# Grouping matrix products by width in the out-projection and the FFN of a Hymba-style decoder layer

## The chip, the core and the metric

The kernel runs on one core of one Trainium2 chip. The core has a matrix engine (TensorE, called PE in the profile; its loads of the stationary operand are a lane of their own, PEld), a vector engine (VectorE, DVE), an engine for activation functions (ScalarE, ACT), a general-purpose engine (GpSimd, POOL) and SyncE (SP), which issues most of the transfers. Each engine works through its own queue in program order and waits on semaphores for the others. The metric is the device time of one execution in microseconds (us); of several runs the median is taken.

## The reference

One decoder layer, float32, 256 tokens, model width 1024:

```python
h = rms_norm(x, norm1_g[l])
proj = h @ w_in[l]
...
x = x + jnp.concatenate([attn, conv], axis=-1) @ w_out[l]
h = rms_norm(x, norm2_g[l])
x = x + (jax.nn.silu(h @ w_gate[l]) * (h @ w_up[l])) @ w_down[l]
```

`attn` is softmax attention of 8 heads of width 64 with RMS-normed, rotated queries and keys (one block of 256 keys, so plain causal attention); `conv` is a gated causal convolution over 31 taps with layer norm and swish. `w_out` is 1024x1024, `w_gate` and `w_up` are 1024x2816, `w_down` is 2816x1024.

## The kernel before, in words

Activations are kept transposed, channels on the 128 partitions and the 256 tokens along the free axis. TensorE reads float32 operands in a rounded form (type fp32r), so each float32 operand is split into a rounded high part and a remainder, the low part. A product is then high times high, plus low weight times high activation, plus high weight times low activation.

**Weights.** They come in blocks of 2048 columns by DMA into `raw` (4 buffers) and are split in pieces of 1024 columns: ACT writes the high part `wh` (line 195), DVE the low part `wl` (line 199), 7 buffers of each. `feed` issues these some 4 pieces ahead of the products that use them.

**Three ways of multiplying.** In the input projection (line 609) all products have 512 moving columns. In the out-projection `mm3s` (line 223 on) takes the four channel tiles of one half and issues twelve 256-column products into a 256-column bank `po`: `wh` and `wl` against the high activations `mixh` in turn, then four `wh` against the low part `mixl`. In the FFN `mm2` (line 207) takes, per weight tile, one product of 512 columns, `wh` against high and low activations side by side (line 210), and one of 256 columns, `wl` against the high activations (line 211). The bank's two halves are added later by `halves` (ACT copies one half, DVE adds).

**The stretch around the change.** The out-projection runs in two halves (attention channels, then convolution channels), each with 8 output tiles d. After each d, DVE adds the bank to the residual `x2T` (line 671). In the second half `x2_task` follows: ACT writes the high part of the FFN's input `g` (line 645) and squares for the norm (647), POOL sums the squares (649), DVE writes the low part of `g` (line 652). The layer norm of the convolution (`bn_stats` to `nb`, lines 564 to 569), its transposes `cT` on TensorE and the split into `mixh` and `mixl` (lines 180, 181) lie inside the first half. Then the FFN: 22 column tiles f, each with 8 gate products into `fg` and 8 up products into `fu`; `norm2_task` puts two matrix steps among them, `pss` (sum of the squares over partitions, in f = 0) and `prb` (line 692, transposes of `wide`, the second norm's factor that DVE has just worked out, lines 685 to 688; between gate and up of f = 1). Last the down projection: 8 tiles d with 22 pairs of products each into `pd`; the last tile takes all its 512-column products in a row (line 764) and its 256-column ones after them into `pdl` (line 773).

**What sets the order.** Python generators (`spawn`, `step`) that are advanced at fixed places of the loops; `keep_order` then fixes the order on each engine as it was written. There are 4 banks of the kind `mm` in PSUM, taken in turn by `po`, `fg`, `fu` and `pd`.

Of the kernel before, what the change touches and what calls it, by code (L numbers as in the profile page):

```python
# [9 lines left out]
F32R = mybir.dt.float32r  # L10
# [3 lines left out]
ALU = mybir.AluOpType  # L14
AX = mybir.AxisListType

P = 128
D = 1024
T = 256
NT = T // P  # L20
KT = D // P
# [4 lines left out]
NF = FF // P  # L26
# [5 lines left out]
PIECE = 1024  # L32
# [4 lines left out]
LEAD = 4  # L37
# [87 lines left out]
def _build(nc, tc, t, ctx):  # L125
# [9 lines left out]
    def mm_bank(name, cols=512):  # L135
        return psum.tile([P, cols], F32, name=name, tag="mm", bufs=4)
# [16 lines left out]
    now = [0]  # L153

    def spawn(gen, wait=0):
        tasks.append([now[0] + wait, gen])

    def step():
        for task in list(tasks):
            while task in tasks and task[0] <= now[0]:  # L160
                try:
                    task[0] = now[0] + next(task[1])
                except StopIteration:
                    tasks.remove(task)
        now[0] += 1
# [37 lines left out]
    def wtile(col, width):  # L203
        j, c = divmod(col, PIECE)
        return [p[:, c:c + width] for p in pieces[j]]

    def mm2(out, w, both, start, stop):


        nc.tensor.matmul(out.rearrange("p (a q) -> p a q", a=2), w[0], both, start=start, stop=False)  # L210
        nc.tensor.matmul(out[:, 0:T], w[1], both[:, 0, :], start=False, stop=stop)  # L211

    def halves(out, bank, side):

# [8 lines left out]
    def mm3s(out, pairs):  # L223

        ops = [(l[a], r[0]) for l, r in pairs for a in range(2)] + [(l[0], r[1]) for l, r in pairs]
        for a, (l, r) in enumerate(ops):
            nc.tensor.matmul(out, l, r, start=a == 0, stop=a == len(ops) - 1)  # L227

    def seed(y, v):

# [41 lines left out]
        nc.tensor.matmul(warm[:, 0:T], zeros[:, 0:P], zeros, start=True, stop=True)  # L272


    xh = keep.tile([P, KT, T], F32R, name="xh", tag="big_h")
    xl = keep.tile([P, KT, T], F32R, name="xl", tag="big_l")
    def split_x(kt):
        nc.scalar.activation(xh[:, kt, :], xT[kt], AF.Copy, scale=g1[:, kt:kt + 1])
        yield
# [338 lines left out]
    mix = G["mix"] = [keep.tile([P, KT, T], F32R, name="mix" + s, tag="big_" + s) for s in "hl"]  # L618
    O = [None, None]
    for h in range(H):  # L620
        feed(unit // 2 + LEAD)
# [33 lines left out]
    for half in range(2):  # L655
        for d in range(KT):
            step()
            feed(off // PIECE + (LEAD if half == 0 or d < OUT_LATE else LEAD - 1))
            if half == 1 and d == 0:
                early_ctx.close()  # L660
                late = ffn["late"] = pool("late")
                xg = late.tile([P, 2, KT, T], F32R, name="g2")
                ffn["h"], ffn["l"] = xg[:, 0], xg[:, 1]
                ffn["acc"] = late.tile([P, T], F32, name="acc")
            b = mm_bank(f"po{half}{d}", T)
            pairs = []
            for a in range(4):
                pairs.append((wtile(off, P), [m[:, 4 * half + a, :] for m in mix]))
                off += P
            mm3s(b, pairs)  # L670
            nc.vector.tensor_tensor(x2T[:, d, :], b, x2T[:, d, :], op=ALU.add)
            if half:
                spawn(x2_task(d))

# [38 lines left out]
    for f in range(NF):  # L713
        pg = t_bank("fg2", "s") if f == 2 else mm_bank(f"fg{f}")
        pu = mm_bank(f"fu{f}")
        order = [(z, k) for z in range(2) for k in range(KT)]
        if f == 0:
            order = [(z, k) for z in range(2) for k in range(KT - 2)]
            order += [(z, k) for k in range(KT - 2, KT) for z in range(2)]
        for a, (z, k) in enumerate(order):  # L720
            if a % 4 == 0:
                if f == a == 0:
                    step()
                feed((off + a * P) // PIECE + LEAD)
                if f or a:
                    step()
            if f and a == 2 * KT // 2:
                spawn(glu_task(f, pg, pu))
                ffn["up"][f] = now[0] + 2
            w = wtile(off + (z * KT + k) * P, P)  # L730
            mm2((pg, pu)[z], w, xg[:, :, k, :], k == 0, k == KT - 1)
        if f == 0:
            spawn(glu_task(0, pg, pu), GLU0_WAIT)
            ffn["up"][0] = now[0] + GLU0_WAIT
        off += 2 * KT * P
# [15 lines left out]
    for d in range(KT):  # L751
        b = mm_bank(f"pd{d}")
        lows = []
        for f in range(NF):
            if f % 4 == 0:
                feed(off // PIECE + LEAD)
                step()
            w = wtile(off, P)
            off += P
            if d < KT - 1:  # L760
                mm2(b, w, acts[:, :, f, :], f == 0, f == NF - 1)
            else:
                both = b.rearrange("p (a q) -> p a q", a=2)
                nc.tensor.matmul(both, w[0], acts[:, :, f, :], start=f == 0, stop=f == NF - 1)  # L764
                lows.append(w[1])
        if d < KT - 1:
            for _ in out_task(d, b):
                pass
# [60 lines left out]
```

## Time and profile before

| | |
|---|---|
| median of 3 runs | 302.23 us (301.79 to 303.49) |
| profiled execution | 301.46 us, of which the span of the program's instructions is 299.3 us |
| PE busy | 292.5 us (98% of the span) |
| DVE busy | 222.6 us (74%) |
| ACT busy | 173.1 us (58%) |
| DMA | 56.6 MB, mean 189 GB/s |

Busy times are unions: matmuls overlap, so the busy time of a group is more than what it adds to the span. What a matmul adds is the distance from its start to the next one's. Rows of a timeline give the start in us from the span's start, the length, engine, line, operation, what is written from what, shapes, and in brackets the idle time before it with what ended it; consecutive equal rows are merged (x22), and then the length runs from the first start to the last end. In the chain of waits the length of a merged row is the time that it adds to the chain.

### The profile page before, as it was taken

To read this page: it belongs to the slowest core of one execution; us is meant where nothing else is said; L and a number is where in the kernel's file an instruction comes from. 1 tells how busy PE (TensorE), PEld (TensorE's weight loads), DVE (VectorE), ACT (ScalarE), POOL (GpSimd) and SP (SyncE) were. 2 spreads that over 40 slices of the span, in tenths; PEclk is the share of its full clock that TensorE was granted. 3 is DMA by queue.
4 is the path that set the end of the run, shared out by engine and by line. 5 is a ranking of instruction groups with operands and counts; after the bars stand their busy time and mean duration, and the time that the engine had idled before them with its cause. 6 is when DMAs were issued, how large, how long until landed. Compare 5 with 4: busy or idle time off the path is not lost.

```text
span 299.3 us, 4415 instructions
## 1 busy us (share of the span) xinstructions
PE 292.5 (98%) x1663; PEld 249.0 (83%) x1663; DVE 222.6 (74%) x414; ACT 173.1 (58%) x303; POOL 21.2 (7%) x41
## 2 busy tenths in 40 slices
PE   8999999999799999999999999999999999999994
PEld 5888877777599998888888888888888888888884
DVE  3799986999847999788888887787787666455312
ACT  6776759897607683566666665665665544344000
POOL 0006380000000170000000000000000000000000
PEclk9999999999999999999999999999999999999999
DMA  7999769346504437456474655644644636530000
GB/s 258 418 416 360 301 257 333 143 140 205 219 0 142 157 126 279 143 163 258 153 251 160 234 189 162 242 159 158 235 171 152 233 120 242 185 124 18 18 20 18
DMA packets 10759, 56.59 MB, mean 189 GB/s; under 512 B 1457, under 2 KB 3089, under 8 KB 4850
## 3 DMA queue, kind: packets, MB, share of 16 engines
q1 hardware_dynamic: 10306, 54.86, 50.4%
q0 software_dynamic: 288, 1.45, 1.4%
q8 instruction: 13, 0.21, 0.3%
q14 instruction: 8, 0.07, 0.1%
q10 hardware_dynamic: 144, 0.00, 0.0%
HBM read 55.26 MB, written 1.05 MB: 188 GB/s over the span
## 4 chain that ended last, share of the span: by engine, by line
PE 96%; DVE 2%; issue 0%
PE p L609 18%; PE fg L210 14%; PE fu L210 14%; PE pd L210 12%; PE po L227 8%; PE fu L211 7%; PE fg L211 7%; PE pd L211 6%; PE pd L764 2%; PE warm L272 1%; PE S L458 1%; PE pT L488 1%; PE pdl L773 1%; PE O L629 1%; PE cv L219 1%; PE cv L221 0%
## 5 line engine op out<-in xcount | busy, mean ns | idle before, releaser
L199 DVE TENSOR_TENSOR wl<-raw,wh 128x1024 fp32r<-128x1024 f32 x90 | 109.3, 1230 | 0.0
L195 ACT ACTIVATE wh<-raw 128x1024 fp32r<-128x1024 f32 x90 | 93.1, 1048 | 8.0 <-PE pd L210 3.3
L210 PE MATMUL fu<-g,wh 128*128 128x512 f32 x176 | 63.3, 399 | 0.0
L210 PE MATMUL fg<-g,wh 128*128 128x512 f32 x176 | 63.3, 399 | 0.0
L210 PE MATMUL pd<-act,wh 128*128 128x512 f32 x154 | 54.5, 399 | 0.0
L211 PE MATMUL fu<-g,wl 128*128 128x256 f32 x176 | 49.4, 281 | 0.0
L211 PE MATMUL fg<-g,wl 128*128 128x256 f32 x176 | 49.4, 281 | 0.0
L211 PE MATMUL pd<-act,wl 128*128 128x256 f32 x154 | 43.2, 281 | 0.0
L210 PEld LDWEIGHTS fu<-g,wh 128*128 128x128 f32 x176 | 33.1, 188 | 8.2
L210 PEld LDWEIGHTS fg<-g,wh 128*128 128x128 f32 x176 | 33.1, 188 | 8.1
L210 PEld LDWEIGHTS pd<-act,wh 128*128 128x128 f32 x154 | 28.9, 188 | 7.3
L211 PEld LDWEIGHTS fu<-g,wl 128*128 128x128 f32 x176 | 33.2, 189 | 0.0
L211 PEld LDWEIGHTS fg<-g,wl 128*128 128x128 f32 x176 | 33.2, 189 | 0.0
L609 PE MATMUL p<-wh,xh 128*128 128x512 f32 x80 | 32.7, 409 | 0.0
L609 PE MATMUL p<-wh,xl 128*128 128x512 f32 x80 | 31.4, 393 | 0.0
L211 PEld LDWEIGHTS pd<-act,wl 128*128 128x128 f32 x154 | 29.1, 189 | 0.0
L609 PE MATMUL p<-wl,xh 128*128 128x512 f32 x80 | 26.5, 392 | 0.0
L216 DVE TENSOR_TENSOR o<-pd,os 128x256 f32<-128x256 f32 x8 | 3.4, 424 | 29.4 <-ACT os L215 29.4
L701 ACT ACTIVATE sf<-tg 128x256 f32<-128x256 f32 x22 | 9.2, 419 | 24.0 <-DVE tg L699 24.0
L215 ACT ACTIVATE os<-pd 128x256 f32<-128x256 f32 x8 | 3.1, 385 | 34.0 <-PE pd L211 29.4
L706 ACT ACTIVATE act<-ac 128x256 fp32r<-128x256 f32 x22 | 9.2, 418 | 20.9 <-DVE ac L705 20.9
L216 DVE TENSOR_TENSOR ac<-fu,us 128x256 f32<-128x256 f32 x22 | 9.3, 424 | 14.5 <-ACT us L215 14.5
(157 smaller groups left out, 406.5 us busy)
## 6 DMA issues: line engine op xcount, KB each, us to landing
raw<-w SPq DMA_DIRECT2D x45, 1024.0 KB, 4.8
first<-first SPq DMA_DIRECT2D x8, 384.0 KB, 5.9
xtok<-xtok SPq DMA_DIRECT2D x2, 512.0 KB, 9.3
x2T<-xT SPq DMA_DIRECT2D x1, 1024.0 KB, 7.3
out<-o SPq DMA_DIRECT2D x8, 128.0 KB, 1.7
inv<-inv POOLq DMA_DIRECT2D x1, 768.0 KB, 6.9
fwd<-fwd POOLq DMA_DIRECT2D x1, 648.0 KB, 4.1
c_glub<-glub SPq DMA_DIRECT2D x1, 512.0 KB, 9.6
```

What stands on the lines that cost most here:

```text
L195: nc.scalar.activation(dst[0], src, AF.Copy)
L199: nc.vector.tensor_tensor(dst[1], src, dst[0].bitcast(F32), op=ALU.subtract)
L210: nc.tensor.matmul(out.rearrange("p (a q) -> p a q", a=2), w[0], both, start=start, stop=False)
L211: nc.tensor.matmul(out[:, 0:T], w[1], both[:, 0, :], start=False, stop=stop)
L215: nc.scalar.activation(side, bank[:, T:], AF.Copy)
L216: nc.vector.tensor_tensor(out, bank[:, 0:T], side, op=ALU.add)
L219: nc.tensor.matmul(out, lhs[0], rhs[0], start=start, stop=False)
L227: nc.tensor.matmul(out, l, r, start=a == 0, stop=a == len(ops) - 1)
L609: nc.tensor.matmul(banks[i], (xh, xh, xl)[a][:, kt, sls[i]], w[a % 2], start=kt == 0 and a == 0, stop=kt == KT - 1 and a == 2 - (order[-1] ...
L701: nc.scalar.activation(s, tg, AF.Silu)
L706: nc.scalar.activation(acts[:, 0, f, :], ac, AF.Copy)
L764: nc.tensor.matmul(both, w[0], acts[:, :, f, :], start=f == 0, stop=f == NF - 1)
```

## The change

`mm2` now takes a list of jobs (weight tile, activations, bank): it issues the 512-column products of all of them, then all their 256-column products. In the gate and up products a list holds 8 tiles (in f = 0 first 12, six of gate and six of up, then 4); in the down projection 8, 8 and 6. The out-projection uses the same routine with lists of 4: the twelve 256-column products of a d become four of 512 and four of 256 columns, the bank `po` is 512 columns wide, and DVE adds its two halves to `x2T` one after the other. For that `mixh` and `mixl` become halves of one tile, as do `xh` and `xl`, whose memory they take over.

```diff
-    def mm2(out, w, both, start, stop):
-        nc.tensor.matmul(out.rearrange("p (a q) -> p a q", a=2), w[0], both, start=start, stop=False)
-        nc.tensor.matmul(out[:, 0:T], w[1], both[:, 0, :], start=False, stop=stop)
+    def mm2(jobs, first, last):
+        seen, left = set(), {}
+        for z, out, w, both in jobs:
+            left[z] = left.get(z, 0) + 1
+            nc.tensor.matmul(out.rearrange("p (a q) -> p a q", a=2), w[0], both, start=z in first and z not in seen,
+                             stop=False)
+            seen.add(z)
+        for z, out, w, both in jobs:
+            left[z] -= 1
+            nc.tensor.matmul(out[:, 0:T], w[1], both[:, 0, :], start=False, stop=z in last and left[z] == 0)
...
-            b = mm_bank(f"po{half}{d}", T)
-            pairs = []
+            b = mm_bank(f"po{half}{d}")
+            jobs = []
             for a in range(4):
-                pairs.append((wtile(off, P), [m[:, 4 * half + a, :] for m in mix]))
+                jobs.append((d, b, wtile(off, P), mixed[:, :, 4 * half + a, :]))
                 off += P
-            mm3s(b, pairs)
-            nc.vector.tensor_tensor(x2T[:, d, :], b, x2T[:, d, :], op=ALU.add)
+            mm2(jobs, (d,), (d,))
+            for a in range(2):
+                nc.vector.tensor_tensor(x2T[:, d, :], b[:, a * T:(a + 1) * T], x2T[:, d, :], op=ALU.add)
...
-            w = wtile(off + (z * KT + k) * P, P)
-            mm2((pg, pu)[z], w, xg[:, :, k, :], k == 0, k == KT - 1)
+                jobs.append((z, (pg, pu)[z], wtile(off + (z * KT + k) * P, P), xg[:, :, k, :]))
+                a += 1
+            mm2(jobs, (0, 1) if f or g == 0 else (), (0, 1) if f or g else ())
...
+        for g, n in ((0, 8), (8, 8), (16, 6)):
+            jobs = []
+            for f in range(g, g + n):
...
+                jobs.append((d, b, wtile(off, P), acts[:, :, f, :]))
```

TensorE's queue at the gate products of f = 1 and the two transposes `prb` behind them. Before, the end of the gate products and the start of the up products (`fg` and `fu` are their banks, `g` the FFN's input):

```order
L210 MATMUL fg_1376<-g_1144,wh_1181 128x512
L211 MATMUL fg_1376<-g_1144,wl_1182 128x256
L210 MATMUL fg_1376<-g_1144,wh_1181 128x512
L211 MATMUL fg_1376<-g_1144,wl_1182 128x256
L692 MATMUL prb<-c_ident,wide 128x128 x2
L210 MATMUL fu_1377<-g_1144,wh_1225 128x512
L211 MATMUL fu_1377<-g_1144,wl_1226 128x256
```

The same place now:

```order
L214 MATMUL fg_1326<-g_1118,wh_1149 128x512 x8
L219 MATMUL fg_1326<-g_1118,wl_1150 128x256 x8
L696 MATMUL prb<-c_ident,wide 128x128 x2
L214 MATMUL fu_1327<-g_1118,wh_1187 128x512 x8
L219 MATMUL fu_1327<-g_1118,wl_1188 128x256 x8
```

The transposes stand where they stood, between the gate and the up products of f = 1; the products on both sides are grouped.

VectorE's queue at the end of the out-projection's second half, d = 4 to 7. Before (`x2T` is the residual, `g` the low part of the FFN's input, `wl` a low part of weights, here that of f = 1's up products):

```order
L671 TENSOR_TENSOR x2T<-po_1229,x2T 128x256
L652 SCALAR_TENSOR_TENSOR g_1144<-x2T,c_cols,g_1144 128x256
L671 TENSOR_TENSOR x2T<-po_1248,x2T 128x256
L652 SCALAR_TENSOR_TENSOR g_1144<-x2T,c_cols,g_1144 128x256
L671 TENSOR_TENSOR x2T<-po_1267,x2T 128x256
L652 SCALAR_TENSOR_TENSOR g_1144<-x2T,c_cols,g_1144 128x256
L671 TENSOR_TENSOR x2T<-po_1286,x2T 128x256
L652 SCALAR_TENSOR_TENSOR g_1144<-x2T,c_cols,g_1144 128x256 x2
L199 TENSOR_TENSOR wl_1226<-raw_860,wh_1225 128x1024
```

The same place now:

```order
L675 TENSOR_TENSOR x2T<-po_1191,x2T 128x256 x2
L655 SCALAR_TENSOR_TENSOR g_1118<-x2T,c_cols,g_1118 128x256
L675 TENSOR_TENSOR x2T<-po_1207,x2T 128x256 x2
L655 SCALAR_TENSOR_TENSOR g_1118<-x2T,c_cols,g_1118 128x256
L675 TENSOR_TENSOR x2T<-po_1223,x2T 128x256 x2
L655 SCALAR_TENSOR_TENSOR g_1118<-x2T,c_cols,g_1118 128x256
L675 TENSOR_TENSOR x2T<-po_1239,x2T 128x256 x2
L655 SCALAR_TENSOR_TENSOR g_1118<-x2T,c_cols,g_1118 128x256 x2
L199 TENSOR_TENSOR wl_1188<-raw_859,wh_1187 128x1024
```

Each addition to `x2T` is now two, the second on what the first wrote; everything else on VectorE stands in the order in which it stood.

## Rows read from the trace of the kernel before

**Rows 1.** The page: busy time of each engine, and the shares of the chain that ended last.

```profile
PE 292.5 (98%) x1663; PEld 249.0 (83%) x1663; DVE 222.6 (74%) x414; ACT 173.1 (58%) x303; POOL 21.2 (7%) x41
...
PE 96%; DVE 2%; issue 0%
```

**Rows 2.** Busy time of each engine by stretch (us from the span's start), then granted clock of TensorE, share of the DMA engines and GB/s: out-projection in two parts, the seam to the FFN, gate and up, down.

```profile
84.00:97.00 13.00, 13.00 (x109) 12.91 (x109) 8.63 (x26) 5.70 (x10) 0.00 (x0) 1.00 0.24 82
97.00:110.00 13.00, 13.00 (x106) 12.77 (x106) 12.68 (x23) 9.92 (x21) 5.69 (x6) 1.00 0.46 163
110.00:122.00 12.00, 12.00 (x73) 10.45 (x72) 10.79 (x24) 5.91 (x9) 1.20 (x2) 1.00 0.62 214
122.00:233.00 111.00, 111.00 (x630) 96.29 (x629) 88.35 (x145) 69.52 (x124) 0.00 (x0) 1.00 0.53 190
233.00:287.00 54.00, 54.00 (x308) 46.80 (x307) 28.26 (x39) 19.32 (x25) 0.00 (x0) 1.00 0.34 124
```

**Rows 3.** TensorE's timeline at the first product of the down projection's pairs, and the two runs of one width that follow.

```profile
233.21 0.40 PE L210 MATMUL pd<-act,wh 128*128 128x512 f32 x1
...
287.62 5.18 PE L764 MATMUL pd<-act,wh 128*128 128x512 f32 x22
292.63 2.79 PE L773 MATMUL pdl<-act,wl 128*128 128x256 f32 x22
```

**Rows 4.** The chain of waits in order of time, runs of products of one width: 512 columns in the input projection (6 and 12 in a row, between transposes), 256 in the out-projection, 512 and 256 at the end.

```profile
33.22 1.38 PE p L609 x6
...
59.33 2.77 PE p L609 x12
...
93.98 14.39 PE po L227 x120
...
287.79 5.01 PE pd L764 x22
292.80 2.64 PE pdl L773 x22
```

**Rows 5.** TensorE's timeline in the convolution, the fourth and the last of its eighteen 512-column products in a row.

```profile
80.79 0.39 PE L219 MATMUL cv<-yh,inv 128*128 128x512 f32 x1
...
84.07 0.39 PE L221 MATMUL cv<-yh,inv 69*128 69x512 f32 x1
```

**Rows 6.** Groups of instructions: count | busy us, mean ns of one | idle time before.

```profile
L210 PE MATMUL fu<-g,wh 128*128 128x512 f32 x176 | 63.3, 399 | 0.0
L210 PE MATMUL fg<-g,wh 128*128 128x512 f32 x176 | 63.3, 399 | 0.0
L210 PE MATMUL pd<-act,wh 128*128 128x512 f32 x154 | 54.5, 399 | 0.0
...
L671 DVE TENSOR_TENSOR x2T<-po,x2T 128x256 f32<-128x256 f32 x16 | 6.3, 415 | 4.5 <-PE po L227 4.5
```

**Rows 7.** DVE's timeline from the first addition of the out-projection to the second norm's factor.

```profile
85.94 0.42 DVE L671 TENSOR_TENSOR x2T<-po,x2T 128x256 f32<-128x256 f32 x1 [4.53 <-PE po L227]
...
95.34 0.69 DVE L181 TENSOR_TENSOR mixl<-cs,mixh 128x512 fp32r<-128x512 f32 x1 [1.06 <-ACT mixh L180]
96.91 0.69 DVE L181 TENSOR_TENSOR mixl<-cs,mixh 128x512 fp32r<-128x512 f32 x1 [0.88 <-ACT mixh L180]
97.52 1.22 DVE L199 TENSOR_TENSOR wl<-raw,wh 128x1024 fp32r<-128x1024 f32 x1
...
101.50 0.48 DVE L652 SCALAR_TENSOR_TENSOR g<-x2T,c_cols,g 128x256 fp32r<-128x256 f32 x1 [0.30 <-ACT g L645]
...
107.94 0.41 DVE L671 TENSOR_TENSOR x2T<-po,x2T 128x256 f32<-128x256 f32 x1
108.28 0.63 DVE L652 SCALAR_TENSOR_TENSOR g<-x2T,c_cols,g 128x256 fp32r<-128x256 f32 x1
108.83 0.41 DVE L671 TENSOR_TENSOR x2T<-po,x2T 128x256 f32<-128x256 f32 x1
109.16 1.51 DVE L652 SCALAR_TENSOR_TENSOR g<-x2T,c_cols,g 128x256 fp32r<-128x256 f32 x2
110.60 4.03 DVE L199 TENSOR_TENSOR wl<-raw,wh 128x1024 fp32r<-128x1024 f32 x3
114.55 0.15 DVE L685 TENSOR_SCALAR v<-pss 128x2 f32<-128x2 f32 x1
...
116.70 0.29 DVE L688 COPY wide<-rstd 128x256 f32<-128x256 f32 x1
```

**Rows 8.** DVE's timeline, two operations of 128x256 of which the second reads what the first wrote.

```profile
119.51 0.41 DVE L216 TENSOR_TENSOR tg<-fg,gs 128x256 f32<-128x256 f32 x1
119.96 0.43 DVE L699 TENSOR_TENSOR tg<-tg,r_bc 128x256 f32<-128x256 f32 x1
```

**Rows 9.** TensorE's timeline at the seam to the FFN: the sixth gate tile of f = 0, the two steps of the second norm, and the product before and after `prb`.

```profile
109.98 0.40 PE L210 MATMUL fg<-g,wh 128*128 128x512 f32 x1
...
112.45 0.50 PE L683 MATMUL pss<-one,acc 128*128 128x1 f32 x4
...
116.94 0.28 PE L211 MATMUL fg<-g,wl 128*128 128x256 f32 x1
117.06 0.42 PE L692 MATMUL prb<-c_ident,wide 128*128 128x128 f32 x2
117.24 0.48 PE L210 MATMUL fu<-g,wh 128*128 128x512 f32 x1
```

More of the change, by code (lines that the diff above doesn't have):

```diff
@@ L221, in mm3 @@
         nc.tensor.matmul(out, lhs[1], rhs[0], start=False, stop=stop)
[L223 to L227, printed above, removed]
     def seed(y, v):
@@ L272, in _build @@
         nc.tensor.matmul(warm[:, 0:T], zeros[:, 0:P], zeros, start=True, stop=True)
-    xh = keep.tile([P, KT, T], F32R, name="xh", tag="big_h")
-    xl = keep.tile([P, KT, T], F32R, name="xl", tag="big_l")
+    xhl = keep.tile([P, 2, KT, T], F32R, name="xhl", tag="big")
+    xh, xl = xhl[:, 0], xhl[:, 1]
     def split_x(kt):
@@ L617, in _build @@
     nc.vector.tensor_scalar(vs[:, 1, :], banks[1], rstd1[:, 1:2], None, op0=ALU.mult)
-    mix = G["mix"] = [keep.tile([P, KT, T], F32R, name="mix" + s, tag="big_" + s) for s in "hl"]
+    mixed = keep.tile([P, 2, KT, T], F32R, name="mix", tag="big")
+    mix = G["mix"] = [mixed[:, 0], mixed[:, 1]]
     O = [None, None]
@@ L715, in _build @@
         pu = mm_bank(f"fu{f}")
-        order = [(z, k) for z in range(2) for k in range(KT)]
+        groups = [[(z, k) for k in range(KT)] for z in range(2)]
         if f == 0:
[L718 to L729, printed above, removed]
-            w = wtile(off + (z * KT + k) * P, P)
-            mm2((pg, pu)[z], w, xg[:, :, k, :], k == 0, k == KT - 1)
+            groups = [[(z, k) for z in range(2) for k in range(KT - 2)],
+                      [(z, k) for k in range(KT - 2, KT) for z in range(2)]]
+        a = 0
+        for g, group in enumerate(groups):
+            jobs = []
+            for z, k in group:
+                if a % 4 == 0:
+                    if f == a == 0:
+                        step()
+                    feed((off + a * P) // PIECE + LEAD)
+                    if f or a:
+                        step()
+                if f and a == KT:
+                    spawn(glu_task(f, pg, pu))
+                    ffn["up"][f] = now[0] + 2
+                jobs.append((z, (pg, pu)[z], wtile(off + (z * KT + k) * P, P), xg[:, :, k, :]))
+                a += 1
+            mm2(jobs, (0, 1) if f or g == 0 else (), (0, 1) if f or g else ())
         if f == 0:
@@ L753, in _build @@
         lows = []
[L754 to L759, printed above, removed]
-            if d < KT - 1:
[L761 to L764, printed above, removed]
+        for g, n in ((0, 8), (8, 8), (16, 6)):
+            jobs = []
+            for f in range(g, g + n):
+                if f % 4 == 0:
+                    feed(off // PIECE + LEAD)
+                    step()
+                jobs.append((d, b, wtile(off, P), acts[:, :, f, :]))
+                off += P
+            if d < KT - 1:
+                mm2(jobs, (d,) if g == 0 else (), (d,) if g + n == NF else ())
+                continue
+            both = b.rearrange("p (a q) -> p a q", a=2)
+            for f, (_, _, w, act) in enumerate(jobs, g):
+                nc.tensor.matmul(both, w[0], act, start=f == 0, stop=f == NF - 1)
                 lows.append(w[1])
```

## The prediction, made before the changed kernel ran

> **What bounds the kernel now.** Read first the page's busy times and the chain of waits [rows 1]: PE is busy 98% of the span and carries 96% of the chain, DVE 2%. So only what changes PE's own pace, or makes PE wait where it does not wait now, can change the time. Second, the busy times by stretch [rows 2]: PE never stands still from 84 to 287 us, at a granted clock of 1.00, which is 2.4 GHz. DVE, though, is nearly full beside it at one place: 12.68 of 13.0 us from 97 to 110 and 10.79 of 12.0 from 110 to 122, against 80% in the gate and up products and about half in the down projection. That is the second half of the out-projection and the seam to the FFN, and the change gives DVE work just there. Third, starts of products. Where 512 and 256 columns alternate, 154 pairs take 287.62 - 233.21 = 54.41 us, or 353.3 ns a pair [rows 3, 6]; in the gate and up products 630 records in 111 us give 352 [rows 2]. A run of 256-column products takes 14.39/120 = 119.9 ns each, and 2.64/22 = 120.0; a run of 512-column ones 1.38/6 = 230, 2.77/12 = 231 and 5.01/22 = 227.7 [rows 4], but (84.07 - 80.79)/14 = 234.3 in the convolution [rows 5]. Fourth, DVE's own timeline through the seam [rows 7].
>
> **Part 1: grouping on PE.** No column is added or taken away in the FFN. A pair in a group costs one product of a 512 run and one of a 256 run. Eight in a row is close to the runs of 6 and 12, so I take 230.5 + 120.0 = 350.5 ns, 2.8 less than 353.3. Bounds: the long run's 227.7 gives 347.7 (5.6 less), the convolution's 234.3 gives 354.3 (1.0 more). How many pairs count? Those after the point where PE waits in part 3, which is `prb`: gate and up are 352 pairs [rows 6], of which 16 (f = 0) and 8 (gate of f = 1) lie before it, and the down projection adds 154: 328 + 154 = 482 pairs. Gain 482 x 2.8 = 1.35 us; bounds -0.5 and +2.7. The last down tile already has its runs apart and keeps its time.
>
> **Part 2: out-projection on PE.** Per d, 12 x 120 = 1440 ns become 4 x 230.5 + 4 x 120 = 1402: 0.6 us over 16 d. It lies before the wait of part 3 and is swallowed by it, so I count nothing.
>
> **Part 3: the added additions on DVE.** Each d now has two additions to `x2T`: 16 more. One that reads what the operation before it wrote starts 119.96 - 119.51 = 0.447 us after it, the 0.41 of the row and the pause for its result [rows 8], while one that needs nothing of its neighbour lets the next start after 108.28 - 107.94 = 0.34 [rows 7]. The second addition reads the first one's result, so each pair puts 0.447 more into DVE's queue: 16 x 0.447 = 7.15 us. What can absorb it is DVE's idle time between the first addition (85.94) and `wide` (116.70). The 4.53 us before 85.94 are no help, since nothing is ready then. Behind it stand 1.06, 0.88 and 0.30 us in front of the two `mixl` and the first `g` [rows 7], 2.24 in all; I add 0.08 for each, since a back-to-back successor starts 0.08 before its forerunner ends (96.91 + 0.69 against 97.52). That makes 2.5. The rest, 7.15 - 2.5 = 4.6 us, is delay of everything behind in DVE's queue: the low parts of `g`, three `wl`, `v` from `pss`, the Newton steps, `wide`. Bounds: if the second addition costs only 0.34, 16 x 0.34 - 2.5 = 2.9; if the eight in the second half are stretched by POOL's sums as the `g` operations beside them are (0.63 against 0.48), 1.2 more, 5.8. I take 4.6, since the additions at 107.94 and 108.83, with POOL busy, took 0.41 like the rest.
>
> PE feels this at three places. First, at the start of the second half, where a 512-column product needs `mixl` at once: the additions ahead of it have made DVE late, and PE waits about 1 us. Second, in f = 0: the low part of the sixth tile of `g` is ready at 108.28 + 0.63 = 108.91 now, used by PE at 109.98 [rows 7, 9]: 1.07 us of slack. Fifteen of the additions lie before it, 15 x 0.447 - 2.5 = 4.2: ready at 113.1. PE, which gets there at about 109.4, waits, and because the 256-column products now stand behind all twelve of 512, it has nothing to fill the wait with. From there 7 x 0.2305 + 12 x 0.12 = 3.05 us lead to `pss`, at 116.2 instead of 112.45, and 12 more pairs and `pss` itself to `prb` at about 120.7. Third, `prb` itself: `wide` ends now at 116.99 and `prb` starts at 117.06, with PE arriving just then (116.94 + 0.12), so there is no slack [rows 7, 9]. `wide` will end at 116.99 + 4.6 = 121.6, PE waits some 0.9 us more, and `prb` starts 4.6 us later than now. This last wait includes the first two; nothing is added up. The weights are no further loss: the `wl` of f = 1's up products, the first of the three from 110.60, would be ready about 116.5, for use after 121.7.
>
> **Part 4: what costs nothing.** One tile for `mixh` and `mixl`, or `xh` and `xl`, changes addresses and names. ACT and POOL keep their rows; they follow DVE's `x2T` and are later with it, hidden by the same wait. The transfers of weights are issued as `wl` operations free their buffers, hence 4.6 us later with PE just as late. Behind `prb` nothing on PE waits now, so nothing there can be shortened but the pace.
>
> **Sum.** +4.6 - 1.35 = +3.25 us. The profiled execution would go from 301.46 to 304.7. That execution is 0.77 below the median of the runs, so the median goes from 302.23 to 305.5.
>
> **Rivals.**
> *The pace of the long run from the first product on.* 227.7 ns in every group: gain 2.7, sum +1.9, median 304.1. For it: the last tile's run, which also starts behind a pair. Against: the runs of 6 and 12 took 230 and 231.
> *No gain from grouping.* The 512-column products keep the convolution's 234.3, and the order brings nothing: sum +4.6 to +5.1, median 307.1. For it: eighteen in a row there never became faster. The Trainium skill, "TensorE: Matmul & The Clock Gate", section "Back-to-back issue gap", gives a warm gap of N/2.4 + 2.5 ns by the columns of a product alone, in which the neighbour's width has no place; by it the order gains nothing and the sum would be +4.6. The trace disagrees with its level (an estimate by that page's rule is 215.8 and 109.2 ns, against 227.7 and 120.0 measured), and no run here shows yet whether the order matters.
> *The seam is cheap.* The second addition starts 0.34 after the first, delay 2.9; sum +1.5, and the result is no slower than can be told from no change if the pace gains a little more than I think. It decides from a delay at `prb` below 2.85 us. Against: rows 8.
> *Pace by columns alone, the kernel faster.* From 120.0 to 227.7 the 256 further columns cost 107.7 ns, so a pair's 768 columns are worth 323 ns, and 30 ns of a pair are fixed. Were a group to lose most of that, 482 x 30 = 14.5 would outweigh the seam: median 292.3. The place is every group behind `prb`, and it decides from 4.6/482 = 9.5 ns a pair. Against: the runs are groups already, and lose at most 5.6.
>
> **How the numbers follow.** Forecast 0.50; long-run pace 0.20; no gain 0.16; cheap seam 0.10; columns alone 0.04. A change of less than 0.5% (1.5 us) can't be told from none here. Of the forecast 0.02, of the long-run pace 0.08 and of the cheap seam 0.05 fall within it, 0.15 together; faster is the last rival and 0.01 of the cheap seam, 0.05; the rest, 0.80, is slower. The forecast's own range is 304.2 to 306.8 (delay 4.0 to 5.2, gain 0.7 to 2.0). With the neighbours it is 303.3 to 307.4, which leaves the cheap seam's lower half and the last rival outside.
>
> **What would show it.** Right: DVE with no idle from 86 to `wide`; `prb` near 121.7; PE waits before the fourth to sixth product of f = 0 and at `prb`; from `prb` on a pair at 350 to 351 ns, so that the down projection's 154 pairs take 54.0 us instead of 54.4. Wrong: `prb` before 120 (the additions cost less, or DVE had room that I did not see), or a pair behind it under 345.

## The result, and the profile of the changed kernel

The changed kernel takes 306.22 us (median of 4 runs, 304.89 to 306.70), the kernel before 302.01 in the same comparison (4 runs, 300.49 to 303.49): a ratio of 1.0148 with a 95% interval of 1.0113 to 1.0183. It is slower; the prediction said 305.5, in a range from 303.3 to 307.4. Ratios and intervals, here and below, leave out executions over 1.5% above the fastest of their kernel, while medians are of all, so the two can differ.

The profiled execution took 306.70 us with a span of 304.6, 5.2 more than that of before. First the page: the busy times, and the chain that ended last by engine.

```profile
PE 294.6 (97%) x1599; PEld 249.1 (82%) x1599; DVE 229.0 (75%) x430; ACT 173.1 (57%) x303; POOL 20.8 (7%) x41
...
PE 79%; DVE 18%; ACT 1%; issue 1%; DVEq 0%
```

Against [rows 1] DVE has gone from 2% of the chain to 18%: for a stretch it, and not PE, sets the time. Its busy time grew by 6.4 us. The stretch is seen in DVE's timeline, from the first addition to the second norm's factor `wide`, the same stretch as [rows 7].

```profile
87.74 0.88 DVE L675 TENSOR_TENSOR x2T<-po,x2T 128x256 f32<-128x256 f32 x2 [4.49 <-PE po L219]
...
97.17 1.67 DVE L675 TENSOR_TENSOR x2T<-po,x2T 128x256 f32<-128x256 f32 x4
98.75 1.28 DVE L181 TENSOR_TENSOR mix<-cs,mix 128x512 fp32r<-128x512 f32 x2
99.95 1.22 DVE L199 TENSOR_TENSOR wl<-raw,wh 128x1024 fp32r<-128x1024 f32 x1
...
110.88 0.87 DVE L675 TENSOR_TENSOR x2T<-po,x2T 128x256 f32<-128x256 f32 x2
111.66 0.47 DVE L655 SCALAR_TENSOR_TENSOR g<-x2T,c_cols,g 128x256 fp32r<-128x256 f32 x1
112.05 0.88 DVE L675 TENSOR_TENSOR x2T<-po,x2T 128x256 f32<-128x256 f32 x2
112.84 0.90 DVE L655 SCALAR_TENSOR_TENSOR g<-x2T,c_cols,g 128x256 fp32r<-128x256 f32 x1
...
116.87 4.03 DVE L199 TENSOR_TENSOR wl<-raw,wh 128x1024 fp32r<-128x1024 f32 x3
120.82 0.15 DVE L689 TENSOR_SCALAR v<-pss 128x2 f32<-128x2 f32 x1
...
122.97 0.29 DVE L692 COPY wide<-rstd 128x256 f32<-128x256 f32 x1
```

No row behind the first has a bracket, nor has one of those left out: DVE waits no more, its pauses between operations are all under 0.06 us, and the gaps of 1.06, 0.88 and 0.30 us of [rows 7] are gone. From the first addition to the end of `wide` it takes 122.97 + 0.29 - 87.74 = 35.52 us, where it took 116.99 - 85.94 = 31.05 before: 4.47 more. Taken apart by starts, the additions and the pauses behind them take 7.1 us more. What DVE had idle gives back 2.3. Another 0.3 comes from the operations beside POOL's sums: one `wl` that took 1.76 before takes 1.21 now (0.55 less), and the low parts of `g` take 0.2 more.

TensorE's timeline at the seam to the FFN, which answers to [rows 9], shows what that does to PE, and the busy times by stretch beside it (PE, PEld, DVE, ACT, POOL, then the granted clock, share of the DMA engines and GB/s) what the clock does.

```profile
99.58 1.25 PE L214 MATMUL po<-mix,wh 128*128 128x512 f32 x4 [0.71 <-DVE mix L181]
...
112.06 1.16 PE L214 MATMUL fg<-g,wh 128*128 128x512 f32 x4 [0.95 <-POOL acc L652]
113.80 0.50 PE L214 MATMUL fg<-g,wh 128*128 128x512 f32 x1 [0.58 <-DVE g L655]
114.99 0.66 PE L214 MATMUL fg<-g,wh 128*128 128x512 f32 x1 [0.68 <-DVE g L655]
115.45 2.76 PE L214 MATMUL fu<-g,wh 128*128 128x512 f32 x6
...
119.70 0.50 PE L687 MATMUL pss<-one,acc 128*128 128x1 f32 x4
...
124.33 0.38 PE L696 MATMUL prb<-c_ident,wide 128*128 128x128 f32 x2
```

```profile
77.00:79.00 2.00, 1.61 (x13) 1.42 (x15) 2.00 (x4) 0.64 (x2) 0.00 (x0) 0.66 0.93 393
79.00:81.00 2.00, 2.00 (x15) 1.62 (x13) 1.57 (x4) 0.60 (x1) 0.00 (x0) 0.50 0.06 25
...
113.00:115.00 2.00, 0.73 (x3) 0.20 (x2) 1.97 (x5) 1.20 (x4) 1.20 (x2) 1.00 0.00 0
115.00:117.00 2.00, 2.00 (x5) 1.61 (x6) 1.97 (x5) 1.63 (x5) 1.02 (x2) 0.54 0.00 0
117.00:119.00 2.00, 2.00 (x10) 1.71 (x10) 2.00 (x2) 2.00 (x3) 0.54 (x1) 0.60 0.00 0
119.00:121.00 2.00, 2.00 (x16) 1.87 (x15) 1.97 (x3) 0.42 (x1) 0.00 (x0) 1.00 0.53 160
```

PE stands still three times in f = 0 (the first of the FFN's column tiles), for 0.95, 0.58 and 0.68 us, and right behind that the granted clock falls to 0.54 and 0.60 of 2.4 GHz, that is to the 1.2 GHz level for most of four microseconds. So `prb` starts at 124.33, 1.07 after the end of `wide` at 123.26. Before, it started 0.07 after it [rows 7, 9]. From the first addition to `prb` it is 36.58 us, against 31.12.

Behind `prb` the change pays. The first groups of the down projection in TensorE's timeline, and the last tile, which answer to [rows 3]:

```profile
239.08 2.00 PE L214 MATMUL pd<-act,wh 128*128 128x512 f32 x8
240.92 1.12 PE L219 MATMUL pd<-act,wl 128*128 128x256 f32 x8
241.87 2.00 PE L214 MATMUL pd<-act,wh 128*128 128x512 f32 x8
...
292.88 5.18 PE L775 MATMUL pd<-act,wh 128*128 128x512 f32 x22
```

Eight pairs take 241.87 - 239.08 = 2.79 us, or 349 ns each, and all 154 pairs (292.88 - 239.08)/154 = 349.4, against 353.3. From `prb` to the end of the span it is 304.58 - 124.33 = 180.25 us, where it was 299.33 - 117.06 = 182.27: 2.02 gained.

So the 5.25 us between the two profiled spans are: +1.80 ahead of the first addition (87.74 against 85.94), +4.47 on DVE, +0.99 by which `prb` is later behind `wide`, -2.02 behind `prb`. The first of the four isn't the change's: the two stretches from 77 to 81 us show the clock at or near half in the attention products `O`, behind a wait of PE. Another execution of the kernel before has the same (b1_again, below), and another one of the changed kernel doesn't: its clock stays at 1.00 there, and its first addition starts at 86.56 (a1_again). From the first addition on the profiles differ by 3.44 us, the medians by 4.2.

### The profile page after: what moved, and what is told of

Its sections match the earlier page's. It is cut to its first block, busy times and chain, and to the rows that moved or that the text cites. A ratio compares the mean times of both kernels' runs of the same rounds, so it can differ in the third digit from the quotient of the medians.

```text
span 304.6 us, 4311 instructions
## 1 busy us (share of the span) xinstructions
PE 294.6 (97%) x1599; PEld 249.1 (82%) x1599; DVE 229.0 (75%) x430; ACT 173.1 (57%) x303; POOL 20.8 (7%) x41
## 3 DMA queue, kind: packets, MB, share of 16 engines
HBM read 55.26 MB, written 1.05 MB: 185 GB/s over the span
## 4 chain that ended last, share of the span: by engine, by line
PE 79%; DVE 18%; ACT 1%; issue 1%; DVEq 0%
PE fu L214 14%; PE fg L214 13%; PE p L611 12%; PE pd L214 12%; PE fg L219 7%; PE fu L219 7%; PE pd L219 6%; DVE wl L199 5%; DVE x2T L675 3%; PE pd L775 2%; DVE p L486 1%; PE warm L274 1%; DVE g L655 1%; DVE sm L469 1%; PE O L632 1%
## 5 line engine op out<-in xcount | busy, mean ns | idle before, releaser
L611 PE MATMUL p<-wh,xhl 128*128 128x512 f32 x160 | 47.7, 402 | 0.0
L214 PE MATMUL fg<-g,wh 128*128 128x512 f32 x176 | 45.3, 396 | 2.2 <-DVE g L655 1.3
L214 PE MATMUL fu<-g,wh 128*128 128x512 f32 x176 | 45.7, 401 | 0.0
L214 PE MATMUL pd<-act,wh 128*128 128x512 f32 x154 | 38.9, 393 | 0.0
L611 PEld LDWEIGHTS p<-wh,xhl 128*128 128x128 f32 x160 | 29.8, 189 | 6.7 <-issue 0.7
L611 PE MATMUL p<-wl,xhl 128*128 128x512 f32 x80 | 26.6, 393 | 0.0
L219 PEld LDWEIGHTS fu<-g,wl 128*128 128x128 f32 x176 | 24.1, 190 | 1.7
L219 PE MATMUL fg<-g,wl 128*128 128x256 f32 x176 | 25.1, 284 | 0.0
L219 PE MATMUL fu<-g,wl 128*128 128x256 f32 x176 | 24.8, 283 | 0.0
L219 PE MATMUL pd<-act,wl 128*128 128x256 f32 x154 | 21.8, 283 | 0.0
```

What stands on the lines that cost most here:

```text
L611: nc.tensor.matmul(banks[i], (xh, xh, xl)[a][:, kt, sls[i]], w[a % 2], start=kt == 0 and a == 0, stop=kt == KT - 1 and a == 2 - (order[-1] ...
```

## The experiments

Each row is read from the profile of that kernel as above, in us: start of the first addition; from there to the end of `wide`, and to `prb`; from `prb` to the end of the span; the sum of the last two, which leaves the front of the program out; and the ns of a pair in the down projection.

| kernel | first addition | to end of `wide` | to `prb` | `prb` to end | sum | pair | median us (runs) |
|---|---|---|---|---|---|---|---|
| before | 85.94 | 31.05 | 31.12 | 182.27 | 213.39 | 353.3 | 302.01 (4) |
| changed | 87.74 | 35.52 | 36.58 | 180.25 | 216.83 | 349.4 | 306.22 (4) |
| e1_ffn_only | 86.46 | 31.05 | 31.11 | 180.31 | 211.42 | 349.4 | 299.99 (12) |
| e2_out_only | 86.39 | 35.53 | 35.59 | 182.31 | 217.90 | 353.3 | 306.51 (4) |
| e3_one_add | 86.74 | 30.86 | 31.20 | 180.26 | 211.46 | 349.4 | 300.52 (10) |
| e4_f0_pairs | 86.31 | 35.53 | 35.59 | 180.33 | 215.92 | 349.4 | 304.61 (9) |
| e5_groups_of_4 | 86.24 | 35.51 | 36.44 | 180.89 | 217.33 | 350.2 | 305.69 (1) |
| e6_spare_adds | 86.53 | 34.21 | 34.26 | 182.28 | 216.54 | 353.3 | 305.80 (4) |
| e7_scan | 88.15 | 31.05 | 31.12 | 184.53 | 215.65 | 353.3 | 305.93 (1) |
| e8_fillers | 86.99 | 35.53 | 35.58 | 180.30 | 215.88 | 349.4 | 304.99 (9) |
| a1_again (changed) | 86.56 | 36.19 | 37.84 | 180.25 | 218.09 | 349.4 | 306.78 (1) |
| b1_again (before) | 88.19 | 31.05 | 31.12 | 182.30 | 213.42 | 353.3 | 303.74 (1) |

**The two halves of the change, each alone.** e1 is the changed kernel with the out-projection of before: `mm3s`, 256-column banks, one addition.

```diff
-            mm2(jobs, (d,), (d,))
-            for a in range(2):
-                nc.vector.tensor_tensor(x2T[:, d, :], b[:, a * T:(a + 1) * T], x2T[:, d, :], op=ALU.add)
+            mm3s(b, pairs)
+            nc.vector.tensor_tensor(x2T[:, d, :], b, x2T[:, d, :], op=ALU.add)
```

> The FFN and the down projection grouped as in the changed kernel, the out-projection as before (twelve 256-column products, one addition). My theory: grouping is worth 353.3 - 349.2 = 4.1 ns for each of the 482 pairs behind prb, and nothing ahead of it, since prb starts when VectorE's wide is done: 2.0 us faster than before, about 300.0 us, ratio 0.9935. Rival (the pairs are faster in that one profile for another reason than their order): 302, ratio 1.000.

e2 keeps the new out-projection, and in the FFN and the down projection `mm2` works its list off one pair at a time.

```diff
-        for z, out, w, both in jobs:
-            nc.tensor.matmul(...)
+        for c in range(0, len(jobs), size):
+            part = jobs[c:c + size]
...
-            mm2(jobs, (0, 1) if f or g == 0 else (), (0, 1) if f or g else ())
+            mm2(jobs, (0, 1) if f or g == 0 else (), (0, 1) if f or g else (), 1)
```

> The out-projection of the changed kernel (two additions per d), all pairs of the FFN and the down projection alternating as before. My theory: VectorE's queue reaches wide 4.5 us later, prb with it, and nothing is given back: about 306.5 us, ratio 1.015. Rival (the seam's loss comes mostly from the products of f = 0 standing in one group of twelve, with nothing to fill the waits): the alternating products fill them, and the loss is 1 to 2 us, ratio 1.005.

e1 took 299.99 us (299.48 to 301.18), ratio 0.9971 [0.9939, 1.0004]; e2 306.51 (303.74 to 306.86), ratio 1.0126 [1.0070, 1.0183]. The two columns of the table separate cleanly: e1 has all of the gain behind `prb` and nothing of the loss ahead of it, e2 all of DVE's loss and none of the gain. Grouping is worth 182.27 - 180.31 = 1.96 us, the new out-projection costs 35.59 - 31.12 = 4.47. TensorE's timeline of e1 has `prb` within 0.6 us of its place in [rows 9], and 0.06 behind the end of `wide`:

```profile
117.57 0.44 PE L700 MATMUL prb<-c_ident,wide 128*128 128x128 f32 x2
```

e1 is also the version that the experiments point to: faster than the changed kernel by 6 us, and than the kernel before by 2 us (1.97 in the profile from the first addition on, 1.9 by the medians), though its interval just reaches 1.

**Is it the additions?** e3 leaves out the second addition of each d, so the products of `wh` with the low part of the activations don't reach the result; TensorE's work is that of the changed kernel.

```diff
-            for a in range(2):
-                nc.vector.tensor_tensor(x2T[:, d, :], b[:, a * T:(a + 1) * T], x2T[:, d, :], op=ALU.add)
+            nc.vector.tensor_tensor(x2T[:, d, :], b[:, 0:T], x2T[:, d, :], op=ALU.add)
```

> The changed kernel with one addition per d: the bank's second half, high weights times the low part of the activations, is computed but not added, so the output lacks it. My theory (the added additions in VectorE's queue are the loss): wide comes when it came before, and the pace gain is left: about 300.1 us, ratio 0.994. Rival (the 512-column product's early need of mixl, the wider bank, or PE's order is the loss): still over 304, ratio 1.008 or more.

e6 is the opposite: the kernel before, with a second addition of the same size behind the first, into a tile that nobody reads.

```diff
             nc.vector.tensor_tensor(x2T[:, d, :], b, x2T[:, d, :], op=ALU.add)
+            nc.vector.tensor_tensor(spare, b, x2T[:, d, :], op=ALU.add)
```

> The kernel before, with one more addition per d behind the one to x2T: the bank plus the new x2T into a tile that nobody reads. Products, banks and orders are those of before. My theory (VectorE's queue from the first addition to wide is full but for 2.5 us, so 16 additions at 0.447 us shift wide and prb by 4.5): the stretch from the first addition to the end of wide goes from 31.05 to 35.5 us, about 306.4 us, ratio 1.015. Rival (the loss needs the new products and the wider bank as well): less than 2 us, ratio under 1.007.

e3 took 300.52 us (299.89 to 301.88), ratio 0.9975 [0.9945, 1.0006]: without the second additions the seam is as short as before, 30.86 to `wide`, and the pace gain stays. e6 took 305.80 (305.08 to 306.76), ratio 1.0132 [1.0065, 1.0198], so additions alone, with PE's products untouched, make the kernel slower. But they cost 34.21 - 31.05 = 3.16 us there, not 4.47, nor the 4.5 expected. Where the 1.3 us went shows in the groups of DVE from 84 to 124.6 us; first the changed kernel, then e6:

```profile
L675 DVE TENSOR_TENSOR x2T<-po,x2T 128x256 f32<-128x256 f32 x32 | 13.1, 420 | 5.0 <-PE po L219 4.5
L655 DVE SCALAR_TENSOR_TENSOR g<-x2T,c_cols,g 128x256 fp32r<-128x256 f32 x8 | 5.0, 638 | 0.0
```

```profile
L673 DVE TENSOR_TENSOR spare<-po,x2T 128x256 f32<-128x256 f32 x16 | 6.8, 424 | 0.5
L672 DVE TENSOR_TENSOR x2T<-po,x2T 128x256 f32<-128x256 f32 x16 | 6.7, 417 | 4.5 <-PE po L227 4.5
L653 DVE SCALAR_TENSOR_TENSOR g<-x2T,c_cols,g 128x256 fp32r<-128x256 f32 x8 | 3.7, 475 | 0.0
```

The additions cost the same in both (13.1 and 13.5 us busy). It is the low parts of `g` that differ, 5.0 against 3.7 us: 638 ns each against 475. In the kernel before they took 4.8, or 599 each, so e6 wins back there what the changed kernel doesn't. In e6 ACT and POOL need the first addition alone and are through with a tile earlier, so that POOL's sums fall beside other operations of DVE (the last section has rows for that). This is read from the timelines and was not tried by itself.

**What makes PE late at `prb`.** e4 takes f = 0 in pairs again, everything else as in the changed kernel: then PE has a 256-column product to do in the waits.

```diff
-            mm2(jobs, (0, 1) if f or g == 0 else (), (0, 1) if f or g else ())
+            mm2(jobs, (0, 1) if f or g == 0 else (), (0, 1) if f or g else (), 32 if f else 1)
```

> The changed kernel, but the products of f = 0 alternate as before, so that 256-column products stand between the waits for g. My theory: PE reaches prb before wide, as VectorE's queue allows; the 1.07 us by which prb followed wide in the changed kernel's profile, after a stretch at half the granted clock, goes: about 305.2 us, ratio 1.0105, and the granted clock stays near 1.00 through the seam. Rival (PE's order in f = 0 doesn't matter, VectorE alone sets prb): 306.2, ratio 1.014.

e4 took 304.61 us (304.08 to 306.18), ratio 1.0085 [1.0052, 1.0117]. DVE's 35.53 us stay, but PE is there first, `prb` follows `wide` within 0.06, and in all four stretches from 113 to 121 us the clock is at 1.00.

```profile
121.89 0.44 PE L699 MATMUL prb<-c_ident,wide 128*128 128x128 f32 x2 [0.82 <-DVE wide L695]
```

e2, whose f = 0 alternates too, has the same: waits of 0.95 and 0.56 us, a clock of 1.00, `prb` 0.06 behind `wide`. That leaves open whether the clock or the order made PE late, since e4 changes both. e8 therefore leaves the order alone and puts small products of zeros in front of the three places where PE waits.

```diff
+            for _ in range(idle.get(j, 0)):
+                nc.tensor.matmul(fill[:, 0:T], zeros[:, 0:P], zeros, start=True, stop=True)
...
+                {0: 6, 4: 4, 5: 5} if f == g == 0 else {})
```

> The changed kernel, with small products of zeros (256 columns, into a bank that nobody reads) in front of the three places in f = 0 at which TensorE waited: 6 before the first gate product, 4 before the fifth, 5 before the sixth. Order and widths of all other products stay. Theory 'the clock': the lateness of prb behind wide (1.07 us in the changed kernel's profile) comes from the half clock that follows the waits; with the waits filled the six fu products take 1.4 us in place of 2.56, the granted clock stays 1.00 from 113 to 121 us, prb starts within 0.1 us of the end of wide, and the distance from the first addition to prb is 35.6 us (36.58 before); the time is about 1 us under the changed kernel's, near 305.2. Rival 'the order': TensorE is late because all twelve 512-column products stand ahead of the twelve of 256 and the sixth tile of g holds them all up; then fillers change nothing, prb stays some 1 us behind wide, 36.5 us, and the time stays at 306.2.

Beside it the changed kernel ran once more:

> The changed kernel once more, one look. If the half clock in f = 0 belongs to the waits there and not to one execution, the granted clock falls to about 0.5 to 0.6 again behind the sixth gate product of f = 0, and prb comes about 1 us after the end of wide (36.5 us from the first addition to prb); if it was an accident of the one execution, the clock stays at 1.00 and prb follows wide within 0.1 us (35.6 us). On the front part of the program: if the 1.8 us by which the products po began later (86.1 instead of 84.3 us) come and go between executions, po may begin at 84.3 to 85.1 here.

e8 took 304.99 us (304.25 to 306.20), ratio 1.0143 [1.0100, 1.0187]. By the medians it lies 2.9 us above the kernel before measured beside it (302.08), e4 2.7, and the changed kernel 4.2. Its timeline of TensorE and its stretches:

```profile
113.05 0.51 PE L216 MATMUL fg<-g,wh 128*128 128x512 f32 x1
113.40 0.72 PE L215 MATMUL fill<-zeros 128*128 128x256 bf16 x5
114.23 0.50 PE L216 MATMUL fg<-g,wh 128*128 128x512 f32 x1
114.57 1.55 PE L216 MATMUL fu<-g,wh 128*128 128x512 f32 x6
...
122.57 0.44 PE L698 MATMUL prb<-c_ident,wide 128*128 128x128 f32 x2 [0.40 <-DVE wide L694]
```

```profile
113.00:115.00 2.00, 1.83 (x9) 1.27 (x10) 1.93 (x6) 0.83 (x3) 0.95 (x2) 1.00 0.00 0
115.00:117.00 2.00, 2.00 (x14) 1.79 (x13) 2.00 (x3) 1.99 (x4) 1.34 (x2) 1.00 0.00 0
117.00:119.00 2.00, 2.00 (x16) 1.82 (x15) 2.00 (x3) 1.94 (x3) 0.00 (x0) 1.00 0.31 41
```

With the waits filled the clock stays up, six `fu` products take 1.55 us from the first start to the last end in place of 2.76, PE reaches `prb` before `wide` is done and waits for it, and the distance to `prb` is 35.58. The products of the kernel stand in the same order as in the changed one, and the sixth gate product starts at the same distance from the first addition (27.24 and 27.25 us), so the lateness was the clock's. Nor is that one execution: over the whole span the mean granted clock was 0.986 to 0.994 in all four runs of the changed kernel, but 0.998 or more in seven of the nine of e4 and in six of the nine of e8. The second profile of the changed kernel shows the half clock again, and that it can be worse:

```profile
113.00:115.00 2.00, 1.32 (x4) 1.00 (x4) 1.97 (x5) 1.23 (x4) 1.12 (x2) 0.55 0.00 0
115.00:117.00 2.00, 2.00 (x7) 1.51 (x6) 2.00 (x3) 2.00 (x4) 0.90 (x2) 0.50 0.00 0
117.00:119.00 2.00, 2.00 (x11) 2.00 (x10) 2.00 (x3) 1.25 (x2) 0.00 (x0) 0.50 0.29 41
```

```profile
120.30 0.16 DVE L689 TENSOR_SCALAR v<-pss 128x2 f32<-128x2 f32 x1 [0.59 <-PE pss L687]
```

There the half clock began earlier and reached into `pss`; DVE, done with its three `wl`, waited 0.59 us for it, `wide` came 0.66 later (36.19 against 35.53), and `prb` 1.65 behind that. From the first addition to the end this execution took 218.09 us, 1.26 more than the other one, although the waits are the same 0.95, 0.58 and 0.68 us. The clock costs the changed kernel 0.95 us in one profile (216.83 - 215.88) and 2.21 in the other, and the difference in the medians lies between what the two profiles give: 3.44 and 4.70 above before.

**The pace and the place in the run.** e5 cuts the groups of FFN and down projection from eight to four.

```diff
-                mm2(jobs, (d,) if g == 0 else (), (d,) if g + n == NF else ())
+                mm2(jobs, (d,) if g == 0 else (), (d,) if g + n == NF else (), 4)
```

> The changed kernel with lists of 4 tiles instead of 8 in the FFN from f = 1 on and in the down projection. In the changed kernel's trace a 512-column product costs 233, 236, 229, 232, 231 ns in the first five places of its run and 227 from the sixth on, a 256-column one 113 in the first place and 120 after. If the place in the run sets the cost, a pair costs (930 + 473)/4 = 350.7 ns. If each change from one width to the other has a fixed cost (8/7 of the 4.1 ns saved per pair at eight, so 4.7 per pair of changes), it costs 353.3 - 4.7 x 3/4 = 349.8 ns. If grouping had no part in it, 353.3. The down projection's 154 pairs take 54.0, 53.9 or 54.4 us.

The down projection of e5 in TensorE's timeline:

```profile
237.95 1.09 PE L217 MATMUL pd<-act,wh 128*128 128x512 f32 x4
238.88 0.63 PE L222 MATMUL pd<-act,wl 128*128 128x256 f32 x4
239.35 1.09 PE L217 MATMUL pd<-act,wh 128*128 128x512 f32 x4
```

Four pairs take 1.40 us, and over the 154 it is 350.2 ns a pair, halfway between the two expectations; neither is confirmed. By the starts of the lists, the 82 lists of four in the gate and up products behind `prb` take 351.0 ns a pair (353.6 in the kernel before, 349.4 in the changed one), the 35 of the down projection 350.2, and the lists of two with which its tiles d end 349.4. By either expectation two in a row would cost more than four. (e5's f = 0 is grouped as in the changed kernel, and there too the clock falls, to 0.54 and 0.61, and `prb` is 0.93 behind `wide`.) So most of what grouping gives is there with four in a row (2.6 of 4.2 ns in gate and up, 3.1 of 3.9 in the down projection), but what sets the rest is not the length alone, and stays open. In the changed kernel the starts in the trace, averaged over the groups of eight behind 128 us, give 232.8, 236.4, 228.5, 232.2 and 230.5 ns for the first five 512-column products, 227.0, 226.8 and 226.7 for the last three, and 112.9 for the first 256-column product, some 120 for those behind it. Why the pace improves only from the sixth on stays open.

**The pace of alternating products, and the front.** The times of the kernel before lie between 298.64 and 303.85 us. e7 tried whether alternating products can settle at a better pace: small products of growing width in front of each f shift the stream against whatever it might settle on.

```diff
+        if f > 2:
+            scan = t_bank(f"scan{f}")
+            nc.tensor.matmul(scan[:, 0:8 * f + 1], zeros[:, 0:P], zeros[:, 0:8 * f + 1], start=True, stop=True)
```

> The kernel before, with one small product of 25, 33, ... 169 columns of zeros into a spare bank ahead of the gate products of each f from 3 on, which breaks the alternating stream at another distance each time; nobody reads the bank. In the profile of before the pairs took 346.0 ns from 113.6 to 116.9 us and 353.3 from 117.3 on to the end. Theory A (an alternating stream keeps one of two paces, and how it is entered decides which): some f run at about 346.7 ns a pair and some at 353.3, in one execution. Theory B (the pace belongs to the whole execution or to what the other engines do): all f run at the same pace.

> The kernel before once more, unchanged, for a second profile of it. Its times reach from 298.6 to 303.9 us. Theory A of the run e7_scan: the 482 pairs behind prb run at 353.3 ns or at 346.7, all of them, and the execution is 3.2 us shorter in the second case; what else differs between executions is the clock granted to the products O, which cost 1.8 us more in the changed kernel's profile. Theory B: the pace is 353.3 here too, whatever the time.

e7 took 305.93 us, the added products included, with 353.3 ns a pair in the down projection: no other pace showed there. In the gate and up products every f falls back, behind the small product, into the same three pairs in turn, of 349, 350 and 361 ns, that the kernel before has there. The theory of two paces has nothing for it. b1_again took 303.74, and from the first addition on it is the kernel before to 0.03 us (213.42 against 213.39). Its excess lies in the front, where the stretches show the half clock in `O`, behind a wait of PE for `vs`, the values of the attention, of which DVE writes one half:

```profile
77.00:79.00 2.00, 1.18 (x13) 1.11 (x15) 2.00 (x4) 0.97 (x2) 0.00 (x0) 0.88 0.97 352
79.00:81.00 2.00, 2.00 (x15) 1.63 (x13) 2.00 (x4) 0.60 (x1) 0.00 (x0) 0.50 0.37 156
```

That wait in TensorE's timeline, in b1_again and then in the first profile of the kernel before, whose clock stayed at 1.00 from 75 to 87 us:

```profile
77.82 0.32 PE L630 MATMUL O<-pTs,vs 128*64 128x128 f32 x1 [1.65 <-DVE vs L617]
```

```profile
77.23 0.32 PE L630 MATMUL O<-pTs,vs 128*64 128x128 f32 x1 [1.64 <-DVE vs L617]
```

So times near 303.7 fit the half clock behind the wait for `vs`, which comes in some executions and not in others (here in b1_again, e7 and the first profile of the changed kernel, three of twelve profiles); the 1.8 us at the front of the changed kernel's profile are the same thing. No profile is of an execution near 298.6, and what makes those shorter stays open.

## Why the prediction was right, and where it was not

**Part 3, the additions: right.** 4.6 us of delay were worked out, 4.47 measured, by the mechanism named: 16 additions of 0.447 us less the idle time that DVE had (e2, e3; 7.1 less 2.3 by the timelines, 7.15 less 2.5 in the working, and 0.3 less beside POOL, which the working hadn't). The stretching by POOL that was kept for the upper bound didn't come on top: a low part of `g` already took 0.63 before [rows 7], and the additions kept 0.42. The value that would have misled is e6's, whose 3.16 lies near the rival's 2.9, for the other reason shown there. The rival "the seam is cheap" falls by e2.

**Part 3, PE's places: half right.** The wait at `mixl` was put at about 1 us and took 0.71. In f = 0 the sixth tile of `g` was expected at 113.1; less the 1.80 of the front the sixth product started at 113.19. But it was the third wait there, not the only one: two stand ahead of it, at the first and the fifth product. The first, 0.95 us, is put down to POOL, but what the first gate product must have is its bank, and four banks in turn make that the bank of d = 4. Its second addition ends at 110.88 + 0.87 = 111.75, and the product starts 0.31 later; so it does in e4 and e8, and in e3, with one addition, there is no wait. This is read from the timelines and was not tried by itself. That the change also holds a bank until a second addition was left out of the working.

**The step that failed** is the way of PE from the waits to `prb`: `pss` "at 116.2 instead of 112.45", PE at `prb` "at about 120.7", where it "waits some 0.9 us more". It priced what stands behind the waits at the full clock and put the loss of clock at nothing, without a reason. `pss` came at 119.70 - 1.80 = 117.9, and PE came to `prb` 1.07 us behind `wide`, not ahead of it: `prb` is 5.46 us later than before, not 4.6. e4 and e8, where the clock stays up, have what was forecast: PE waits there for `wide` (0.82 and 0.40 us), and in e8 `pss` comes at 117.39, or 116.3 less the 1.05 us by which its first addition is later than before. The Trainium skill, "TensorE: Matmul & The Clock Gate", section "HAM oscillation — how this bites in real kernels", describes groups of some 2 us of products with waits for DMA between them that are longer than that, after each of which the array starts at half its clock. The trace shows the half clock behind waits of 0.95, 0.58 and 0.68 us, shorter than any in that section, so that page of the Trainium skill names the danger but would not have told that it lies here. The section "Back-to-back issue gap" of the same page of the Trainium skill gives N/1.2 ns at the low clock, by which an estimate for 512 columns is 426.7; the chain of waits of the changed kernel agrees:

```profile
115.65 2.56 PE fu L214 x6
```

which is 2.56/6 = 427 ns each.

**Part 1, the pace: right in kind, too small.** The term was 482 x 2.8 = 1.35 us and measured 2.02 (e1: 1.96). The step is the 230.5 + 120.0 = 350.5 ns for a pair: it took the runs of six and twelve for a group of eight, and the pair came to 349.4, between that and the long run's 347.7. The rival "the pace of the long run from the first product on" is not what happens either: the first of eight cost 232.8 ns. The rival "no gain from grouping" falls by e1: the order of widths does matter, by 3.9 ns a pair. The warm figure by columns alone, N/2.4 + 2.5 ns, of the section "Back-to-back issue gap" of the Trainium skill's "TensorE: Matmul & The Clock Gate", which that section calls the gap of a single product by itself, can't give this difference. "Pace by columns alone" falls too, since 3.9 is well under 9.5 ns a pair.

**Part 2 and part 4: right.** e2 shows no gain from the out-projection's products, since DVE sets the end there; and nothing else was lost behind `prb` (182.31 us to the end in e2, 182.27 before).

**The sum.** From the first addition on +3.25 was forecast, and the profile gives +4.47 + 0.99 - 2.02 = 3.44. That is closer than the steps deserve: a pace gain too small by 0.67 and a clock loss of 0.99 that was missed almost cancelled; that was luck. In the second execution, where the clock cost more, it was 4.70. The median's +4.2 lies between the two. Of the prediction's own signs, DVE without idle time and waits of PE in f = 0 came; `prb` near 121.7, a wait of PE there and a pair of 350 to 351 ns did not.

## What to carry to other kernels

An added operation on an engine that is nearly full beside the bottleneck costs its whole start-to-start time less the idle time of that stretch, however small the engine's share of the whole span; here that was 4.5 us for a saving on TensorE that had been put at 0.6. It also moves what runs beside other engines' operations, which was worth 1.3 us between e6 and the changed kernel. Grouping products by width saved 2 us in the FFN and the down projection, but it takes away what could be done while one operand is late; keep pairs alternating where inputs arrive one by one (e4). And price a wait of TensorE twice: its own length, and the half clock that may follow it.

## What the runs showed of the hardware that was not expected

- The clock fell at the last of three waits of 0.95, 0.58 and 0.68 us in f = 0, in both profiles of the changed kernel and in e5, and how long it stayed at half differed between two executions of one kernel (`prb` 1.07 and 1.65 us behind `wide`). The alternating e2 and e4 have waits of 0.95 and 0.56 or 0.57 at the same place and kept 1.00. Behind a wait of 1.64 to 1.67 us for `vs` it fell in three of twelve profiles.
- Where a sum of POOL and an operation of DVE between SBUF tiles meet, the one that starts second takes longer, up to twice its time; an addition that reads PSUM does not. In the changed kernel's DVE timeline above, the low part of `g` at 112.84 takes 0.90 and the one at 111.66 takes 0.47; POOL's timeline:

```profile
109.97 1.56 POOL L652 TENSOR_TENSOR acc<-acc,sq 128x256 f32<-128x256 f32 x1 [0.44 <-ACT sq L650]
112.73 0.73 POOL L652 TENSOR_TENSOR acc<-acc,sq 128x256 f32<-128x256 f32 x1 [1.20 <-ACT sq L650]
```

A sum, begun at 112.73, lies beside the first and none beside the second. The sum of 1.56 us began behind a `wl` of DVE that ran from 109.74 to 110.95: here the sum is stretched, from 0.73, and the `wl` has its usual 1.21. The addition at 108.83 of [rows 7], which took 0.41, stood within four sums of POOL in the kernel before:

```profile
107.74 3.54 POOL L649 TENSOR_TENSOR acc<-acc,sq 128x256 f32<-128x256 f32 x4 [0.73 <-ACT sq L647]
```

- In the groups of eight a 512-column product costs some 227 ns in place of 228 to 236 only from the sixth in a row on. That is no rule for every run of one width: the eighteen in a row of the convolution kept 234.3 on average from the fourth on [rows 5].
